# Memory keys projected by token instead of by head, and the fourth tile of x loaded one to two memory slices earlier

## The chip, the cores and the metric

One core of one Trainium2 chip. The time is that of one execution on the device in microseconds (us); of several runs the median is given. Engines are called TensorE (PE in the profile, PEld for its weight loads), VectorE (DVE), ScalarE (ACT), GpSimd (POOL) and SyncE (SP). Every engine runs its instructions in the order in which they stand in its queue, and an instruction that waits holds up those behind it.

## What is computed

One layer of a decoder trunk over 1024 tokens of width 2048, in float32. The part that the change touches is group C, in which 4 heads attend to 256 memory tokens:

```
h = rmsnorm(x, ln_g[l]);  proj = h @ w_in[l]
... groups A (spatial gating) and B (gated delta rule) ...
m = rmsnorm(mem, mem_norm_g[l])
mk, mv = jnp.split(m @ w_mem_kv[l], 2, axis=-1)      # 256 x 512 each
scores = einsum('bshd,bmhd->bhsm', cq, mk) * XA_HEAD_DIM ** -0.5
out_c = einsum('bhsm,bmhd->bshd', softmax(scores), mv) * silu(c_z)
x = x + concat(out_a, out_b, out_c) @ w_out[l];  return rmsnorm(x, final_g)
```

## The kernel before

Each float32 operand of a large product is split into a high part, rounded to TensorE's faster float32 form, and the remainder. `triple` makes one product of three matmuls: high by high, high by low, low by high.

The kernel does not issue instructions where they are written. A planner (`Plan`, `issue`) records them, prices each one with a table of costs, runs a simulated clock and puts them into each engine's queue in the order in which they would become ready, with a rank to choose between those that are ready together. So a small edit moves instructions that it doesn't name.

The first stage, some 70 us, projects the memory. For each of 16 slices `k` of the width, `load_kv` brings 128 rows of `w_mem_kv` (512 KB; four buffers: `wraw` twice, `ut` twice), ScalarE scales and casts them to `whi`, and VectorE forms `wlo`. The columns 0 to 511 of a slice make the keys, 512 to 1023 the values. `mh` and `ml` (tiles `gt` and `inv`) are the high and low parts of the transposed memory. Values are made by token: the memory is the stationary operand, two tiles `va[mt]` of 128 tokens by 512 columns (PSUM banks `dn` 0 and 1; the profile writes such a matmul `dn<-whi,gt`). Keys are made by head: the weights are stationary, four tiles `ka[h]` of 128 channels by 256 tokens, in the PSUM banks `acc` 0 to 3 (`acc<-gt,whi`). That is the layout which the attention needs, with channels on the partitions. Since a key's token then lies along the free dimension, the row scale of the memory's norm, `rm`, has to be spread over all partitions: `dg` is a diagonal of it, a product with `ones` makes `rmb`, and VectorE multiplies the four tiles with it. The results are stored (`kv_d`) by DMAs that GpSimd issues.

Between the slices the first tiles of x are prepared. `load_x` issues four loads of 128 tokens through SP, each held back by `behind(...)` until a given memory slice has been multiplied (`kvmark`). `prep` takes the row scale (squares on ScalarE, a small sum on VectorE, an inverse square root on GpSimd), scales the tile, and TensorE transposes it in four groups of four 128 x 128 pieces into two PSUM banks used in turn (`spare`: `dn` 2 and 3); VectorE multiplies them by the norm's gain into `tn`, and the high and low parts go to `ahi` and `alo`. The fourth tile, `x_rows[3]`, lies in the buffers `qT` and `qTw`. For the first two tiles `decay_rows` also makes the sums for the decay, in a free part of a bank (`first_ab`): columns 256 to 383 of `acc` 0 and 1, which the keys leave free. After that the input projection begins, which uses all banks.

The attention stands much later, from about 1198 us on. Before it the stored keys are loaded into `gt` (`mkT`) and the values into `inv` (`mv`), by GpSimd's DMAs, and split into high and low parts.

Of the kernel before, what the change touches and what calls it, by code (L numbers as in the profile page):

```python
# [9 lines left out]
F32 = mybir.dt.float32  # L10
F32R = mybir.dt.float32r
AF = mybir.ActivationFunctionType
ALU = mybir.AluOpType
# [4 lines left out]
P = 128  # L18
D = 2048
KT = D // P  # L20
# [4 lines left out]
NMEM = 256  # L25
GW, DW, XW = 512, 1024, 512
NG, NH, NX = 4, 8, 4
# [33 lines left out]
class Plan:  # L61
# [27 lines left out]
    @contextmanager  # L89
    def rank(self, cls):  # L90
        old, self.cls = self.cls, cls
        yield
        self.cls = old

    @contextmanager
    def behind(self, op):
        old, self.gate = self.gate, op
        yield
        self.gate = old
# [204 lines left out]
def kernel(  # L304
# [21 lines left out]
    x, mem, w_in, out = x[0], mem[0], w_in[0], out[0]  # L326
# [7 lines left out]
    V, S, G, PE, Q = R.dve, R.act, R.pool, R.pe, R.sp  # L334
    rank, behind = R.rank, R.behind

    def C(shape, name, dt=F32):
        return sb.tile(list(shape), dt, name=name, tag=name)[:]

    def DT(shape, name, dt=F32):  # L340
        return dr.tile(list(shape), dt, name=name, tag=name)[:]
# [41 lines left out]
    def tok(ap):  # L383

        return ap.rearrange("p (t c) -> p t c", c=P)
# [14 lines left out]
    et = [C([P, HT], f"et{i}") for i in range(2)]  # L400
    ring = {t: Slots(t, 2, [P, HT]) for t in ("kT", "qT", "vs", "kd", "ai")}
# [10 lines left out]
    rm = [rms[:, i : i + 1] for i in range(2)]  # L412
# [5 lines left out]
    dnr = Ring("dn", 4, [P, HT], pool=ps)  # L418
# [6 lines left out]
    ident, ones, utri = (C([P, P], n) for n in ("ident", "ones", "utri"))  # L425
# [11 lines left out]
    def split_to(hi, lo, src, eng):  # L437
        S.copy(hi, src)
        eng.tensor_tensor(out=lo, in0=src, in1=hi, op=ALU.subtract)

    def mm(a, lhs, rhs, start, stop, cls=9):
        with rank(cls):
            return PE.matmul(a, lhs, rhs, start=start, stop=stop, skip_group_check=True)

    def triple(a, l, r, start, stop, cls=9):

        mm(a, l[0], r[0], start, False, cls)
        mm(a, l[0], r[1], False, False, cls)
        return mm(a, l[1], r[0], False, stop, cls)
# [28 lines left out]
    def row_tiles(tag):  # L478
        return [ring[tag](), ring[tag](), *halves(twin[tag])]

    def rows_of(d, q, tt):
        return d[2 * q : 2 * q + 2, :, tt * 2 * P : (tt + 1) * 2 * P].rearrange("j p n -> p j n")

    def twos_of(t):
        return t.rearrange("p (j n) -> p j n", j=2)
# [11 lines left out]
    def kv_parts(k):  # L497
        n = XW if k == 0 else 2 * XW
        return [slice(i, i + n) for i in range(0, 2 * XW, n)]

    def load_kv(k):
        for i, sl in enumerate(kv_parts(k)[::-1]):
            (S if (k, i) == (0, 0) else Q).dma_start(kvraw[k % 4][:, sl], w_mem_kv[k * P : (k + 1) * P, sl])

    def load_x(tt, tag, after=(None,) * 4):
        x_rows[tt] = row_tiles(tag)
        for c in range(4):
            with behind(after[c] or R.gate), rank(2.8):
                Q.dma_start(x_rows[tt][c], x[tt * P : (tt + 1) * P, c * HT : (c + 1) * HT])
# [16 lines left out]
    va, ka = dnr.bufs[0:2], acc  # L526
    flip = dnr.bufs[2:4]

    def spare():
        turn["dn"] = 1 - turn["dn"]  # L530
        return flip[turn["dn"]]
# [8 lines left out]
    pt = acc[3]  # L540
# [4 lines left out]
    def times_g(o, tp, q):  # L545
        V.tensor_tensor(out=o, in0=tp, in1=bc(gcol[:, 16 + 4 * q : 20 + 4 * q], P), op=ALU.mult)
# [26 lines left out]
    H0 = NT // 2  # L573

    def first_ab(tt):
        return ka[tt][:, NMEM : NMEM + P]

    def decay_rows(a, q, t, start):

        with R.together():  # L580
            for j in range(4):
                k = 4 * q + j
                PE.matmul(a[j * 32 : (j + 1) * 32], abw[:, k * 16 : k * 16 + 32], t[:, j],
                          start=start, stop=q == NQ - 1, skip_group_check=True)

    def put0(tt):
        def put(q, tp):
            t = tok(ring["tn"]())
            with rank(1):
                times_g(t, tp, q)  # L590
            with rank(2):
                split_to(ahq[q][:, tt], alq[q][:, tt], t, V)
            if tt < H0:
                decay_rows(first_ab(tt), q, t, False)
            with rank(5):
                Q.dma_start(rows_of(h0_d, q, tt), twos_of(t.rearrange("p k c -> p (k c)")))

        return put


    kvmark = []
# [5 lines left out]
    for k in range(KT):  # L607
        mh, ml = mhl[k // 4]
        if k >= 4:
            with rank(3):  # L610
                load_kv(k)
        hi, lo = kvhi[k % 2], kvlo[k % 2]
        with rank(2):
            for sl in kv_parts(k)[::-1]:
                raw = kvraw[k % 4][:, sl]
                if k == 0:
                    V.tensor_scalar(hi[:, sl], raw, gcol[:, k : k + 1], None, op0=ALU.mult)
                else:
                    S.activation(hi[:, sl], raw, AF.Copy, scale=gcol[:, k : k + 1])
                V.scalar_tensor_tensor(lo[:, sl], raw, gcol[:, k : k + 1], hi[:, sl], op0=ALU.mult, op1=ALU.subtract)  # L620
        kk = k % 4
        for mt in range(2):
            sl = slice(mt * P, (mt + 1) * P)
            triple(va[mt], (mh[:, kk, sl], ml[:, kk, sl]), (hi[:, XW:], lo[:, XW:]), k == 0, k == KT - 1)
        for h in range(NX):
            sl = slice(h * P, (h + 1) * P)
            triple(ka[h][:, :NMEM], (hi[:, sl], lo[:, sl]), (mh[:, kk], ml[:, kk]), k == 0, False)
        kvmark.append(R.ops[-1])
        if k == 0:
            with behind(kvmark[-1]), rank(2):  # L630
                G.dma_start(abw[:, 0 : KT * 16].rearrange("p (k c) -> p k c", c=16),
                            w_in[:, C_AB : C_AB + 16].rearrange("(k p) c -> p k c", p=P))
        if k in (1, 4, 8):
            with behind(kvmark[-1]):
                mhl.append(spread_mem(len(mhl)))
        if k == 1:
            load_x(0, "vs", kvmark[1:2] * 4)
        if k == 3:
            for mt in range(2):
                V.tensor_copy(rm[mt], row_scale(mem_rows[mt]))  # L640
        if k == 4:
            load_x(1, "kd", kvmark[4:5] * 4)
        if k == 5:
            prep(0, put0(0), spare)
        if k == 7:

            dg, rmb = (ring["E"]()[:, 0:NMEM] for _ in range(2))
            for mt in range(2):
                V.tensor_scalar(dg[:, mt * P : (mt + 1) * P], ident, rm[mt], None, op0=ALU.mult)
            pt = spare()  # L650
            PE.matmul(pt[:, 0:NMEM], ones, dg, start=True, stop=True)
            S.copy(rmb, pt[:, 0:NMEM])
        if k == 9:
            prep(1, put0(1), spare)
            load_x(2, "kT", (kvmark[6], kvmark[7], kvmark[7], kvmark[8]))
        if k == 13:
            load_x(3, "qT", (kvmark[10], kvmark[11], kvmark[11], kvmark[12]))
            with rank(2):
                prep(2, put0(2), spare, (2, 3, 0, 1))

    kv_d = DT([2, NX, P, NMEM], "kvd")
    with rank(1):
        kfs = [t[:, i * NMEM : (i + 1) * NMEM] for t in et for i in range(2)]
        for h in range(NX):
            V.tensor_tensor(out=kfs[h], in0=ka[h][:, :NMEM], in1=rmb, op=ALU.mult)
    for h in range(NX):
        with rank(2.5):
            G.dma_start(kv_d[0, h], kfs[h])
    for mt in range(2):
        t = ring[("ai", "kd")[mt]]()  # L670
        with rank(1):
            S.activation(t, va[mt], AF.Copy, scale=rm[mt])
        with rank(2.5):
            G.dma_start(kv_d[1, :, :, mt * P : (mt + 1) * P].rearrange("h p e -> p h e"), tok(t))
    with rank(2):
        prep(3, put0(3), spare, (2, 3, 0, 1))
    sums0 = ring["xr"].bufs[1][:, 0:HT]
    with rank(2):
        for tt in range(H0):
            S.copy(sums0[:, tt * P : (tt + 1) * P], first_ab(tt))  # L680
# [12 lines left out]
    with rank(3.5):  # L693
        S.activation(nal, nal, AF.Exp)
        V.tensor_scalar(nal, nal, -1.0, None, op0=ALU.mult)
        pt = dnr.bufs[3]
# [1029 lines left out]
    for n, (tag, to) in enumerate((("gt", mkT), ("inv", mv))):  # L1726
        for i in range(NX // 2):
            t = ring[tag](F32R).rearrange("p (h s m) -> p h s m", h=2, s=2)
            G.dma_start(t[:, :, 1].bitcast(F32), kv_d[n, 2 * i : 2 * i + 2].rearrange("h p m -> p h m"))
            with rank(1.5):  # L1730
                split_to(t[:, :, 0], t[:, :, 1], t[:, :, 1].bitcast(F32), V)
            to += [t[:, 0], t[:, 1]]
    xab = [heir(b, f"xa{i}", f"ut{i}", 2 * HT, F32R) for i, b in enumerate(ring["ut"].bufs)]
    xat = [t[:, i * HT : (i + 1) * HT] for t in xab for i in range(2)]
# [186 lines left out]
```

## Time and profile before

| | |
|---|---|
| median of 3 runs | 1589.88 us (1587.89 to 1590.94) |
| the profiled execution | 1590.5 us, span of its instructions 1588.7 us |
| TensorE busy | 1575.6 us, 99% of the span |
| VectorE, ScalarE, GpSimd busy | 81%, 64%, 20% |
| chain of work that ended last | TensorE 98%, DMA 1% |
| DMA | 425.77 MB, 268 GB/s over the span |
| granted TensorE clock | 0.998 |

A row of a timeline gives the start, the time to the end of its last instruction, the engine, line, operation and tiles (out<-in, buffer numbers left out), shapes and count; brackets show how long the engine had been idle and who released it. Nearly all instructions carry the planner's line, L300, so one goes by the names of the tiles. Matmuls overlap: the next one starts before the last one's end.

### The profile page before, as it was taken

To read this page: it belongs to the slowest core of one execution; us is meant where nothing else is said; L and a number is where in the kernel's file an instruction comes from. 1 tells how busy PE (TensorE), PEld (TensorE's weight loads), DVE (VectorE), ACT (ScalarE), POOL (GpSimd) and SP (SyncE) were. 2 spreads that over 40 slices of the span, in tenths; PEclk is the share of its full clock that TensorE was granted. 3 is DMA by queue.
4 is the path that set the end of the run, shared out by engine and by line. 5 is a ranking of instruction groups with operands and counts; after the bars stand their busy time and mean duration, and the time that the engine had idled before them with its cause. 6 is when DMAs were issued, how large, how long until landed. Compare 5 with 4: busy or idle time off the path is not lost.

```text
span 1588.7 us, 25645 instructions
## 1 busy us (share of the span) xinstructions
PE 1575.6 (99%) x8762; PEld 1317.2 (83%) x8762; DVE 1287.4 (81%) x1961; ACT 1016.2 (64%) x2088; POOL 311.7 (20%) x513
## 2 busy tenths in 40 slices
PE   9999999999999999999999999999999999999997
PEld 8878888888888888888888888888888888888886
DVE  5868996989899998997988776777768788688775
ACT  6762685776656788866775667766566864344355
POOL 1200042332402424235343133121000000000001
PEclk9999999999999999999999999999999999999999
DMA  8988868988679868986779775798877779688646
GB/s 305 319 279 278 274 214 306 349 303 268 199 253 345 270 215 283 357 306 219 263 233 356 240 259 188 242 327 257 283 255 260 260 238 355 198 283 294 202 146 238
DMA packets 213219, 425.77 MB, mean 268 GB/s; under 512 B 23112, under 2 KB 58672, under 8 KB 213088
## 3 DMA queue, kind: packets, MB, share of 16 engines
q1 hardware_dynamic: 190464, 367.40, 68.9%
q0 software_dynamic: 21840, 55.40, 10.5%
q8 instruction: 69, 1.13, 0.3%
q10 hardware_dynamic: 784, 1.33, 0.2%
q14 instruction: 62, 0.51, 0.1%
HBM read 335.40 MB, written 88.11 MB: 267 GB/s over the span
## 4 chain that ended last, share of the span: by engine, by line
PE 98%; DMA 1%; DVE 0%; issue 0%; ACTq 0%; ACT 0%; POOLq 0%; POOL 0%; DVEq 0%
PE acc L300 69%; PE dn L300 29%; DMA wraw<-in_w_in_dram 0%; DMA wraw<-in_w_mem_kv_dram 0%; DVE alo L300 0%; DVE zl L300 0%; ACTq L300 0%; ACT y2w L300 0%; DVE tn L300 0%; DVE kd L300 0%; DVE vs L300 0%; DVE inv L300 0%; POOLq L1916 0%; POOL small L300 0%; DVE whi L300 0%
## 5 line engine op out<-in xcount | busy, mean ns | idle before, releaser
L300 PE MATMUL acc<-ahi,whi 128*128 128x512 f32 (+1 forms) x1328 | 455.6, 392 | 0.0
L300 PE MATMUL acc<-ahi,wlo 128*128 128x512 f32 (+1 forms) x904 | 355.0, 393 | 0.0
L300 PEld LDWEIGHTS acc<-ahi,whi 128*128 128x128 f32 x1328 | 247.8, 188 | 47.7
L300 ACT CAST ahi<-raws 128x1024 fp32r<-128x1024 f32 x141 | 147.9, 1049 | 86.7 <-PE dn L300 40.4
L300 PEld LDWEIGHTS acc<-ahi,wlo 128*128 128x128 f32 x904 | 170.0, 188 | 32.6 <-issue 0.2
L300 PE MATMUL acc<-alo,whi 128*128 128x512 f32 (+1 forms) x480 | 187.5, 391 | 0.0
L300 PE MATMUL acc<-ahi,zh 128*128 128x512 f32 x424 | 167.2, 394 | 0.0
L300 PE MATMUL acc<-ahi,zl 128*128 128x512 f32 x424 | 167.2, 394 | 0.0
L300 PE MATMUL acc<-alo,zh 128*128 128x512 f32 x424 | 167.1, 394 | 0.0
L300 ACT CAST whi<-wraw 128x1024 fp32r<-128x1024 f32 (+1 forms) x78 | 80.6, 1033 | 70.4 <-PE acc L300 42.8
L300 DVE TENSOR_TENSOR wlo<-wraw,whi 128x1024 fp32r<-128x1024 f32 (+1 forms) x78 | 93.6, 1200 | 25.5 <-ACT whi L300 22.0
L300 POOL TENSOR_TENSOR small<-small,mhalf 128x1 f32<-128x1 f32 x26 | 16.6, 643 | 491.1 <-DVE small L300 488.9
L300 DVE TENSOR_TENSOR alo<-raws,ahi 128x1024 fp32r<-128x1024 f32 x71 | 87.5, 1233 | 21.9 <-ACT ahi L300 21.7
L300 PEld LDWEIGHTS acc<-alo,whi 128*128 128x128 f32 x480 | 90.3, 188 | 17.4
L300 DVE TENSOR_TENSOR ahi<-raws,ahi 128x1024 fp32r<-128x1024 f32 x70 | 85.4, 1220 | 18.8 <-ACT ahi L300 17.3
L300 DVE TENSOR_TENSOR alo<-y,ahi 128x1024 fp32r<-128x1024 f32 x65 | 79.3, 1220 | 17.4 <-ACT ahi L300 17.1
L300 PEld LDWEIGHTS acc<-ahi,zl 128*128 128x128 f32 x424 | 79.7, 188 | 15.3
L300 PEld LDWEIGHTS acc<-ahi,zh 128*128 128x128 f32 x424 | 79.8, 188 | 15.3
L300 PEld LDWEIGHTS acc<-alo,zh 128*128 128x128 f32 x424 | 79.7, 188 | 15.2
L300 ACT CAST ahi<-y 128x1024 fp32r<-128x1024 f32 x65 | 68.2, 1049 | 37.3 <-PE dn L300 17.6
L300 PE MATMUL dn<-whi,ahi 128*128 128x512 f32 x232 | 77.6, 389 | 0.0
L300 PE MATMUL acc<-whi,ahi 128*128 128x512 f32 x216 | 73.6, 392 | 0.0
(582 smaller groups left out, 3744.8 us busy)
## 6 DMA issues: line engine op xcount, KB each, us to landing
wraw<-in_w_in_dram SPq DMA_DIRECT2D x80, 512.0 KB, 5.1
raws<-sa SPq DMA_DIRECT2D x61, 512.0 KB, 5.3
y<-in_w_in_dram SPq DMA_DIRECT2D x40, 512.0 KB, 5.2
wraw<-in_w_out_dram SPq DMA_DIRECT2D x32, 512.0 KB, 4.9
raws<-h0d SPq DMA_DIRECT2D x29, 512.0 KB, 6.0
y<-sa SPq DMA_DIRECT2D x27, 512.0 KB, 4.8
raws<-sd SPq DMA_DIRECT2D x42, 256.0 KB, 2.9
raws<-hTd SPq DMA_DIRECT2D x16, 512.0 KB, 5.2
```

What stands on the lines that cost most here:

```text
L300: o.fn(*o.args, **o.kw)
```

## The change

Keys are made by token, as the values are: two tiles `ka[mt]` of 128 tokens by 512 columns, with three matmuls each, in `acc` 0 and 1. `acc` 2 and 3 are free, and `first_ab` moves there. The row scale is now one number for each partition, so `dg`, `rmb` and the product that spread it go, and two VectorE instructions scale the keys. They are stored by token (`key_d`). Before the attention TensorE transposes them: two groups of four 128 x 128 pieces, into banks that `dnr` gives, from which the high and low parts are taken. The values' path is the same. And the loads of `x_rows[3]` are written at slice 10, tied to slices 9, 9, 10 and 10, where they were tied to 10, 11, 11 and 12.

```
-        return ka[tt][:, NMEM : NMEM + P]
+        return ka[2 + tt][:, 0:P]
...
-                decay_rows(first_ab(tt), q, t, False)
+                decay_rows(first_ab(tt), q, t, q == 0)
...
-        for h in range(NX):
-            sl = slice(h * P, (h + 1) * P)
-            triple(ka[h][:, :NMEM], (hi[:, sl], lo[:, sl]), (mh[:, kk], ml[:, kk]), k == 0, False)
+        for mt in range(2):
+            sl = slice(mt * P, (mt + 1) * P)
+            triple(ka[mt], (mh[:, kk, sl], ml[:, kk, sl]), (hi[:, 0:XW], lo[:, 0:XW]), k == 0, k == KT - 1)
...
-        if k == 7:
-
-            dg, rmb = (ring["E"]()[:, 0:NMEM] for _ in range(2))
-            for mt in range(2):
-                V.tensor_scalar(dg[:, mt * P : (mt + 1) * P], ident, rm[mt], None, op0=ALU.mult)
-            pt = spare()
-            PE.matmul(pt[:, 0:NMEM], ones, dg, start=True, stop=True)
-            S.copy(rmb, pt[:, 0:NMEM])
...
+        if k == 10:
+            load_x(3, "qT", (kvmark[9], kvmark[9], kvmark[10], kvmark[10]))
         if k == 13:
-            load_x(3, "qT", (kvmark[10], kvmark[11], kvmark[11], kvmark[12]))
...
-        for h in range(NX):
-            V.tensor_tensor(out=kfs[h], in0=ka[h][:, :NMEM], in1=rmb, op=ALU.mult)
-    for h in range(NX):
+    for mt in range(2):
+        with rank(1):
+            V.tensor_scalar(et[mt], ka[mt], rm[mt], None, op0=ALU.mult)
         with rank(2.5):
-            G.dma_start(kv_d[0, h], kfs[h])
+            G.dma_start(key_d[mt], et[mt])
...
+            if n == 0:
+                G.dma_start(raw, key_d[:, :, i * NMEM : (i + 1) * NMEM].rearrange("t p c -> p t c"))
+                d = dnr()
+                with rank(1.5):
+                    for h in range(2):
+                        for m in range(2):
+                            PE.transpose(d[:, (2 * h + m) * P : (2 * h + m + 1) * P], raw[:, m, h * P : (h + 1) * P], ident)
+                src = d.rearrange("p (h m) -> p h m", h=2)
```

What the planner makes of it, at three places. TensorE, one memory slice, the third (tiles 113 to 116 are the banks `acc`, 117 and 118 `dn` 0 and 1). Before:

```order
L300 MATMUL dn_118<-whi_73,inv_133 128x512
L300 MATMUL acc_113<-gt_132,whi_73 128x256
L300 MATMUL acc_113<-inv_133,whi_73 128x256
L300 MATMUL acc_113<-gt_132,wlo_75 128x256
L300 MATMUL acc_114<-gt_132,whi_73 128x256
L300 MATMUL acc_114<-inv_133,whi_73 128x256
L300 MATMUL acc_114<-gt_132,wlo_75 128x256
```

and on in the same way for 115 and 116. Now:

```order
L300 MATMUL dn_118<-whi_73,inv_133 128x512
L300 MATMUL acc_113<-whi_73,gt_132 128x512
L300 MATMUL acc_113<-wlo_75,gt_132 128x512
L300 MATMUL acc_113<-whi_73,inv_133 128x512
L300 MATMUL acc_114<-whi_73,gt_132 128x512
L300 MATMUL acc_114<-wlo_75,gt_132 128x512
L300 MATMUL acc_114<-whi_73,inv_133 128x512
```

Twelve matmuls of 256 columns in four banks have become these six of 512 in two.

TensorE, the transposes of the fourth tile of x, in the beginning of the input projection (matmuls of `ahi` and `alo`; 119 and 120 are `dn` 2 and 3). Before:

```order
L300 MATMUL dn_118<-ahi_65,wlo_76 128x256
L300 MATMUL dn_120<-ident,qTw 128x128 x4
L300 MATMUL dn_119<-ident,qTw 128x128 x4
L300 MATMUL dn_120<-ident,qT_146 128x128 x4
L300 MATMUL dn_119<-ident,qT_147 128x128 x4
L300 MATMUL acc_113<-ahi_65,inv_362 128x256
```

and now:

```order
L300 MATMUL dn_118<-ahi_65,whi_73 128x256
L300 MATMUL dn_119<-ident,qTw 128x128 x4
L300 MATMUL dn_118<-alo_69,whi_73 128x256
L300 MATMUL dn_118<-ahi_65,wlo_75 128x256
L300 MATMUL acc_113<-ahi_65,whi_74 128x256
L300 MATMUL dn_120<-ident,qTw 128x128 x4
L300 MATMUL acc_113<-alo_69,whi_74 128x256
```

The four groups no longer stand in one row: two are shown, the third and the fourth follow 12 and 23 rows behind the second. The first now stands 34 narrow matmuls behind the last matmul of the keys, where it stood behind 54.

ScalarE, the end of the memory's slices (`whi_73` from `ut_84` is slice 14, from `wraw_71` with 1024 columns slice 12; `jk` takes the squares of x's fourth tile). Before:

```order
L300 CAST ahi_65<-tn_88 128x512
L300 ACTIVATE whi_73<-ut_84,gcol 128x1024
L300 CAST ahi_66<-tn_89 128x512
L300 ACTIVATE jk,small_110<-qT_147 128x512
L300 CAST inv_362<-wraw_71 128x768
L300 ACTIVATE whi_74<-ut_85,gcol 128x1024
```

and now:

```order
L300 ACTIVATE jk,small_110<-qTw 128x1024
L300 ACTIVATE kdw<-kdw,small_108 128x512
L300 ACTIVATE whi_73<-ut_84,gcol 128x1024
L300 CAST ahi_65<-tn_90 128x512
L300 CAST inv_363<-wraw_71 128x768
```

All squares of that tile now stand ahead of the casts of slices 14 and 15.

More of the change, by code (lines that the diff above doesn't have):

```diff
@@ L655 @@
             load_x(2, "kT", (kvmark[6], kvmark[7], kvmark[7], kvmark[8]))
+        if k == 10:
+            load_x(3, "qT", (kvmark[9], kvmark[9], kvmark[10], kvmark[10]))
         if k == 13:
-            load_x(3, "qT", (kvmark[10], kvmark[11], kvmark[11], kvmark[12]))
             with rank(2):
                 prep(2, put0(2), spare, (2, 3, 0, 1))
-    kv_d = DT([2, NX, P, NMEM], "kvd")
-    with rank(1):
-        kfs = [t[:, i * NMEM : (i + 1) * NMEM] for t in et for i in range(2)]
-        for h in range(NX):
-            V.tensor_tensor(out=kfs[h], in0=ka[h][:, :NMEM], in1=rmb, op=ALU.mult)
-    for h in range(NX):
+    kv_d = DT([NX, P, NMEM], "kvd")
+    key_d = DT([2, P, XW], "keyd")
+    for mt in range(2):
+        with rank(1):
+            V.tensor_scalar(et[mt], ka[mt], rm[mt], None, op0=ALU.mult)
         with rank(2.5):
-            G.dma_start(kv_d[0, h], kfs[h])
+            G.dma_start(key_d[mt], et[mt])
     for mt in range(2):
@@ L673 @@
         with rank(2.5):
-            G.dma_start(kv_d[1, :, :, mt * P : (mt + 1) * P].rearrange("h p e -> p h e"), tok(t))
+            G.dma_start(kv_d[:, :, mt * P : (mt + 1) * P].rearrange("h p e -> p h e"), tok(t))
     with rank(2):
@@ L1728 @@
             t = ring[tag](F32R).rearrange("p (h s m) -> p h s m", h=2, s=2)
-            G.dma_start(t[:, :, 1].bitcast(F32), kv_d[n, 2 * i : 2 * i + 2].rearrange("h p m -> p h m"))
+            raw = t[:, :, 1].bitcast(F32)
+            if n == 0:
[6 more added lines that the diff above has]
+                src = d.rearrange("p (h m) -> p h m", h=2)
+            else:
+                G.dma_start(raw, kv_d[2 * i : 2 * i + 2].rearrange("h p m -> p h m"))
+                src = raw
             with rank(1.5):
-                split_to(t[:, :, 0], t[:, :, 1], t[:, :, 1].bitcast(F32), V)
+                split_to(t[:, :, 0], t[:, :, 1], src, V)
             to += [t[:, 0], t[:, 1]]
```

## Prediction

> **What bounds the kernel now.** I read the page's chain of work first, then the table of TensorE's waits, then the two stretches that the change touches, instruction by instruction.
>
> ```profile
> PE 98%; DMA 1%; DVE 0%; issue 0%; ACTq 0%; ACT 0%; POOLq 0%; POOL 0%; DVEq 0%
> PE dn L300 <- POOL ones L300: 1.1, 1, 1.1
> PE dn L300 <- DVE whi L300: 0.8, 1, 0.8
> PE dn L300 <- DVE ai L300: 0.6, 1, 0.6
> PE dn L300 <- DVE tn L300: 0.3, 1, 0.3
> PE dn L300 <- DVE inv L300: 0.2, 1, 0.2
> 60.00:80.00 20.00, 19.65 (x151) 18.50 (x150) 18.37 (x37) 14.95 (x26) 6.12 (x9) 1.00 1.05 393
> ```
>
> The reader is to see that TensorE carries 98% of the chain and that its five waits sum to 3.0 us in the whole run. So what counts is how long TensorE's own queue is, and whether the change opens a wait in it. Of the five waits one, 0.3 us for `tn`, stands where the change moves things; it is the missing 0.35 us in the stretch from 60 to 80 us (first column TensorE, then weight loads, VectorE, ScalarE, GpSimd, granted clock, DMA share, GB/s). Since matmuls overlap, a matmul's price here is the distance between starts, not the duration in the second column of a timeline. The sum is made against the profiled execution, 1590.5 us (span 1588.7), which lies 0.6 us above the median of the three runs, 1589.88.
>
> **The keys' matmuls.** The order of both programs differs only in the first sixth or so and around the attention; everywhere else it is the same. In each of 16 slices of memory, twelve matmuls of 256 columns become six of 512.
>
> ```profile
> 18.96 0.28 PE L300 MATMUL acc<-gt,whi 128*128 128x256 f32 x1
> ...
> 20.27 0.29 PE L300 MATMUL acc<-gt,wlo 128*128 128x256 f32 x1
> 20.40 0.40 PE L300 MATMUL dn<-whi,gt 128*128 128x512 f32 x1
> ...
> 21.57 0.39 PE L300 MATMUL dn<-whi,inv 128*128 128x512 f32 x1
> 21.80 0.28 PE L300 MATMUL acc<-gt,whi 128*128 128x256 f32 x1
> ```
>
> Twelve narrow ones (first and last shown) take 20.40 - 18.96 = 1.44 us, six wide ones 21.80 - 20.40 = 1.40 us: 0.04 us a slice. The first two slices run at about half pace:
>
> ```profile
> 7.87 1.19 PE L300 MATMUL dn<-whi,gt 128*128 128x512 f32 x2 [0.82 <-DVE whi L300]
> 10.56 1.05 PE L300 MATMUL acc<-inv,whi 128*128 128x256 f32 x4
> 11.42 0.63 PE L300 MATMUL dn<-wlo,gt 128*128 128x512 f32 x1
> ...
> 12.27 0.63 PE L300 MATMUL dn<-wlo,gt 128*128 128x512 f32 x1
> 13.88 0.62 PE L300 MATMUL dn<-whi,gt 128*128 128x512 f32 x2
> ```
>
> There four narrow ones take 0.86 us (10.56 to 11.42) and two wide ones 0.85 (11.42 to 12.27): nothing to gain. So 14 slices by 0.03 to 0.04 us, 0.4 to 0.6: I take **0.5 us gained**. [...]
>
> **The spread of the row scale.** The product that copied the keys' scale over all partitions goes. It is one instruction that ran as two passes:
>
> ```profile
> 38.85 0.70 PE L300 MATMUL dn<-E,ones 128*128 128x256 f32 x2
> 39.48 0.43 PE L300 MATMUL acc<-tn,abw 128*32 128x128 f32 x8
> ```
>
> From start to start 0.63 us, **0.6 us gained**. With it go two small VectorE products and a ScalarE copy, none on TensorE's path.
>
> **The transposes of the keys before the attention.** Eight are new, in two groups of four. A group of four in such a stream:
>
> ```profile
> 47.40 0.60 PE L300 MATMUL dn<-ident,kd 128*128 128x128 f32 x4
> 47.75 0.48 PE L300 MATMUL dn<-whi,inv 128*128 128x512 f32 x1
> 48.06 0.28 PE L300 MATMUL acc<-gt,whi 128*128 128x256 f32 x1
> ```
>
> The four take 0.35 us and the wide matmul behind them 0.31 instead of 0.23, so 0.43 us a group: **0.9 us lost** for two. Do they wait?
>
> ```profile
> L300 POOL DMA_DIRECT2D gt<-kvd x2: 722/742/763, 1026.6 to 1084.0; - x2
> DMA to landing us min/median/max: 4.1/7.0/7.3
> 1165.94 1.03 PE L300 MATMUL dn<-ident,vs 128*128 128x128 f32 x8
> 1166.73 0.48 PE L300 MATMUL acc<-alo,zh 128*128 128x512 f32 x1
> 1166.57 1.27 ACT L300 ACTIVATE vs<-dn,col 128x512 f32<-128x512 f32 x2 [1.59 <-PE dn L300]
> ```
>
> The keys' loads start at the latest at 1084.0 and land within 7.3 us. In the new order the new transposes follow the `vs` transposes that stand at 1165.94 by seven wide matmuls, so some 75 us after the landing; the two banks they write were read by ScalarE until 1167.84, in two equal parts, the first done near 1167.2, and the first group comes near 1168.4. No wait, by about a microsecond. The reading of the transposes replaces a reading from SBUF on ScalarE and VectorE, same number of instructions, both off the path: nothing. The four stores of scaled keys become two, and their scaling on VectorE two instructions instead of four: priced below with x's tile, which queues behind it.
>
> **The fourth tile of x.** Its four loads are released by the end of memory slices 9 and 10 instead of 10, 11 and 12, so its 16 transposes are placed in four groups between other matmuls instead of in one row. The row before:
>
> ```profile
> 75.18 1.03 PE L300 MATMUL dn<-ident,qTw 128*128 128x128 f32 x8
> 76.56 1.26 PE L300 MATMUL dn<-ident,qT 128*128 128x128 f32 x8 [0.35 <-DVE tn L300]
> 77.58 0.60 PE L300 MATMUL acc<-ahi,inv 128*128 128x256 f32 x3
> 78.02 0.31 PE L300 MATMUL acc<-alo,inv 128*128 128x256 f32 x1
> ```
>
> 2.40 us for 16, with 0.35 us of waiting for VectorE to empty the bank. Four groups at 0.43 us are 1.72: **0.7 us gained**, if the groups don't wait in their new places. The first stands 34 narrow matmuls (34 x 0.12 = 4.1 us) behind the last matmul of the keys. On VectorE its scaling stands behind the two key scalings, a `tn` and an `alo`:
>
> ```profile
> 67.85 1.50 DVE L300 TENSOR_TENSOR et<-acc,E 128x256 f32<-128x256 f32 x4 [0.19 <-PE acc L300]
> 69.87 0.68 DVE L300 TENSOR_TENSOR tn<-dn,gcol 128x512 f32<-128x512 f32 x1
> 73.41 0.88 DVE L300 TENSOR_SCALAR qTw<-qTw,small 128x512 f32<-128x512 f32 x2 [0.46 <-POOL small L300]
> ```
>
> A key scaling over 512 elements isn't in the trace; between the scaling from SBUF (`qTw`, 0.44 a piece) and the product from PSUM (`tn`, 0.68), I take the dearer, since it reads PSUM too. With `alo`, of the same size, at the same 0.68, that is 2 x 0.68 + 0.68 + 0.68 + 0.44 = 3.2 us against 4.1: free by 0.9 us; at the cheaper end by 1.4. The 0.46 us of waiting for GpSimd came from its square root standing behind the stores of keys and values; now it stands ahead of them. If every group waited as the one did, 4 x 0.35 = 1.4 us of gain would be lost; if none does, 0.7 is kept. The number of DMAs on SP's queue is unchanged.
>
> **The sum.** 0.5 + 0.6 + 0.7 - 0.9 = 0.9 us gained: 1590.5 - 0.9 = 1589.6 for an execution like the profiled one, and 1589.88 - 0.9 = 1589.0 for the median. The smallest change that a measurement of this kernel can tell from none is about 0.2%, 3.2 us; the three runs lie 3.1 us apart. So the forecast is no change that can be told.
>
> **Rivals.** (1) *The moved tile waits.* Four waits like the old one turn the 0.7 us gain into 0.7 lost: 1590.4 for the median. For it: VectorE is busy 18.37 of the 20 us from 60 to 80, and the margin above is under a microsecond. Against: the groups are apart, so a bank has some 2 us to be emptied (14 narrow matmuls and 4 transposes) before it is written again.
>
> (2) *The early loads starve the keys: slower.* In the new order ScalarE squares the last half of x's tile ahead of the cast of memory slice 14, and SP issues that half ahead of the load of slice 15.
>
> ```profile
> 45.11 4.03 SPq L300 DMA_DIRECT2D ut<-in_w_mem_kv_dram  x2
> 60.35 0.33 SPq L300 DMA_DIRECT2D qTw<-in_x_dram  x1
> DMA to landing us min/median/max: 5.3/5.6/6.1
> 49.92 0.39 PE L300 MATMUL dn<-whi,gt 128*128 128x512 f32 x1
> 62.23 0.39 PE L300 MATMUL dn<-whi,gt 128*128 128x512 f32 x1
> 62.46 1.15 ACT L300 ACTIVATE whi<-ut,gcol 128x1024 fp32r<-128x1024 f32 x1
> ```
>
> Slice 10 ends where slice 11 starts, at 49.92; two issues and a landing of up to 6.1 us later it is 57. A square of this half, a scaling and the cast follow one another on ScalarE; taken at no more than the cast's 1.15 us each they end at 60.4. Slice 14's first matmul stood at 62.23, so 1.3 us are free after TensorE's own half microsecond of gain. Slice 15's load slips from some 49 to 51 at its issue, and its cast stood at 62.46: free by 5 us. To end over 0.2% slower the landing has to be late by 1.3 + 0.9 + 3.2 = 5.4 us, so it decides from a landing of 11.5 us on, nearly twice the longest seen for this tile; price there 4.1 us, 1593.1 or more.
>
> (3) *The clock drops behind transposes.* The trace has one slow stretch, from 7.87 to 13.88, in which 6.0 us went by for what takes 3.0 at full pace. Were the new transposes to bring on another such stretch, it would cost 3.0 us: 1592.0. Against: the 16 transposes at 75.18 are followed by three narrow matmuls in 0.44 us, and the 8 at 1165.94 by a wide one in 0.31, which is the ordinary step behind transposes. [...]
>
> (4) *More than the sum.* To be faster by over 0.2% the change would have to take 2.3 us more than counted, when only 0.35 us of the waits lies in its reach: 1586.5. That it doesn't do what it says is excluded by the order: 192 narrow matmuls fewer, 96 wide ones and 8 transposes more, one spread fewer.
>
> **How the numbers follow.** The forecast 0.67 (its own range 1588.0 to 1590.0: the terms' bounds of 0.2 us and the repeats); rival (1) 0.19; (2) 0.07; (3) 0.03; (4) 0.04. Predicted time 1589.0. Range 1586.8 to 1592.0: its lower end is the lowest repeat of before, 1587.89, less the 0.9 and the 0.2 of the terms' bounds; its upper end is rival (3)'s, and covers the highest repeat, 1590.94, with the 0.5 us that rival (1) lies above before. Outside stay (4), (2) and what repeats add. Faster by over 0.2%: 0.04, from (4). Slower: 0.08, from (2) and a part of (3). Within: 0.88.
>
> **What would show it.** In the profile after: six key matmuls in 1.40 us a slice; no spread at 38.85; the `qT` groups of four between narrow matmuls, each 0.43 us and without a wait; two `gt` groups near 1167, followed at once by matmuls 0.23 us apart. Wrong would be a wait of TensorE for `whi` between 55 and 65 us (rival 2), for `qTw`, `qT` or `tn` near 70 (rival 1), or spacings of 0.42 us behind transposes (rival 3).

## The result, and the profile after

The changed kernel is slower: 1593.43 us median of 8 runs (1591.17 to 1596.79) against 1588.38 us for the kernel before beside it, a ratio of 1.0029 with a 95% interval of 1.002 to 1.0039. The forecast was 1589.0 with a range up to 1592.0. The profiled execution took 1595.3 us (span 1593.6, granted clock 0.995 instead of 0.998).

TensorE's four longest waits after (engine, tile and who is waited for: us in total, times, longest):

```profile
PE acc L300 <- DVE wlo L300: 1.7, 1, 1.7
PE acc L300 <- ACT whi L300: 1.7, 1, 1.7
PE dn L300 <- DVE whi L300: 1.4, 1, 1.4
PE dn L300 <- POOL ones L300: 1.1, 1, 1.1
```

The first two are new. To see where time went, the same three places are looked up in both timelines: the first matmul of the third memory slice, the first of the input projection, and one near 205 us. From the second to the third both kernels have the same matmuls to do. Before:

```profile
17.49 0.48 PE L300 MATMUL dn<-whi,gt 128*128 128x512 f32 x1
...
68.73 0.28 PE L300 MATMUL dn<-ahi,inv 128*128 128x256 f32 x1
...
204.45 0.39 PE L300 MATMUL acc<-ahi,wlo 128*128 128x512 f32 x1
```

After:

```profile
16.33 0.48 PE L300 MATMUL dn<-whi,gt 128*128 128x512 f32 x1
...
66.97 0.28 PE L300 MATMUL acc<-ahi,inv 128*128 128x256 f32 x1
...
209.58 0.39 PE L300 MATMUL acc<-ahi,wlo 128*128 128x512 f32 x1
```

The memory's projection ends 1.76 us sooner; 1.16 of these stand already at the third slice. Then the same work takes 209.58 - 66.97 = 142.61 us instead of 135.72: 6.89 us lost in this one stretch. Behind it the two run in step, but for 0.96 us at the keys' transposes, and 1.1 us that the changed kernel gains near 625, where it lacks two small waits of before: -1.76 + 6.89 - 1.1 + 0.96 = 5.0, the difference of the spans (4.9). So all of the loss lies in the beginning of the input projection, on whose matmuls the change has no line.

Both new waits stand there (a row's brackets: how long idle, and who released it):

```profile
79.09 0.74 PE L300 MATMUL acc<-ahi,wlo 128*128 128x256 f32 x4 [1.74 <-DVE wlo L300]
...
167.81 0.50 PE L300 MATMUL acc<-ahi,whi 128*128 128x512 f32 x1 [1.72 <-ACT whi L300]
```

And each costs nearly twice its length, as the windows behind them show (third-last column: granted TensorE clock):

```profile
79.70:83.10 3.40, 3.40 (x19) 3.40 (x18) 2.27 (x10) 2.99 (x7) 1.67 (x3) 0.50 1.06 378
...
168.50:171.90 3.40, 3.40 (x10) 2.72 (x10) 3.33 (x5) 2.91 (x4) 0.00 (x0) 0.51 1.05 375
```

From 79.09 us on 21 narrow matmuls take 4.10 us, where the step of 0.119 behind them gives 2.51; from 168.57 on 8 wide ones take 3.44, where the step of 0.233 behind them gives 1.86. So each stretch at half clock cost 1.6 us, and two waits of 1.7 and two such stretches are 6.6 of the 6.89 us. (The stretch holds two smaller terms besides, which nearly cancel: 0.65 us gained at the transposes of x's fourth tile, and some 0.6 us lost in steps that are drawn out between 159.7 and 162.1 us. Some 0.3 us stay unexplained.)

Who is late? For the first wait VectorE's and SP's queues tell it:

```profile
76.87 0.69 DVE L300 TENSOR_TENSOR tn<-dn,gcol 128x512 f32<-128x512 f32 x1 [2.54 <-DMA h0d<-tn]
...
78.08 0.95 DVE L300 TENSOR_TENSOR wlo<-wsbt,whi 128x768 fp32r<-128x768 f32 x1
```

```profile
68.06 0.42 SPq L300 DMA_DIRECT2D h0d<-tn  x1
DMA to landing us min/median/max: 3.8/6.4/8.7
```

The last line is that of the twelve such stores issued between 50 and 86 us; this one is the longest. The `tn` of x's fourth tile reuses one of four buffers, whose store to `h0d` landed only 8.7 us after its issue; the `tn` starts 0.1 us later. The `wlo` that TensorE needs stands behind that `tn`.

For the second wait the same chain is shown in both kernels: SP's load of `kTw`, and VectorE's addition that uses it. Before:

```profile
155.72 0.84 SPq L300 DMA_DIRECT2D kTw<-in_w_in_dram  x2
```

```profile
161.03 0.96 DVE L300 TENSOR_TENSOR wraw<-kTw,wraw 128x768 f32<-128x768 f32 x1
```

After:

```profile
159.82 1.99 SPq L300 DMA_DIRECT2D kTw<-in_w_in_dram  x2
```

```profile
163.64 1.55 DVE L300 SCALAR_TENSOR_TENSOR sct<-sct 128x32 f32<-128x32 f32 x7
165.22 0.19 DVE L300 SCALAR_TENSOR_TENSOR sc<-sct,sc 128x32 f32<-128x32 f32 x1
165.87 0.96 DVE L300 TENSOR_TENSOR wraw<-kTw,wraw 128x768 f32<-128x768 f32 x1 [0.46 <-DMA kTw<-in_w_in_dram]
```

The load is issued 4.1 us later and used 4.8 us later, while TensorE is only 1 us later; seven small `sct` instructions that were spread around the addition now stand ahead of it. VectorE was late before that: its previous addition from `kTw` stands at 157.46 us instead of 154.73, 2.7 us later, and it too waited for its load.

### The profile page after: what moved, and what is told of

The parts are those of the page before. It is cut to its first block, busy times and chain, and to the rows that moved or that the text cites. A ratio compares the mean times of both kernels' runs of the same rounds, so it can differ in the third digit from the quotient of the medians.

```text
span 1593.6 us, 25448 instructions
## 1 busy us (share of the span) xinstructions
PE 1577.3 (99%) x8672; PEld 1313.3 (82%) x8672; DVE 1287.1 (81%) x1957; ACT 1015.5 (64%) x2087; POOL 308.2 (19%) x511
## 3 DMA queue, kind: packets, MB, share of 16 engines
q8 instruction: 68, 1.11, 0.3%
## 4 chain that ended last, share of the span: by engine, by line
PE 92%; DMA 4%; DVE 2%; issue 1%; ACT 0%; POOL 0%; SPq 0%; ACTq 0%; POOLq 0%; DVEq 0%
PE acc L300 64%; PE dn L300 27%; DMA wraw<-in_w_in_dram 1%; DMA kTw<-in_w_in_dram 1%; DVE alo L300 1%; DMA h0d<-tn 1%; DMA kTw<-in_x_dram 0%; DMA vsw<-sa 0%; DMA wraw<-in_w_mem_kv_dram 0%; DVE wlo L300 0%; DVE wraw L300 0%; DMA y<-in_w_in_dram 0%; DVE zl L300 0%; DVE tn L300 0%; ACT whi L300 0%
```

## The experiments

All results are ratios of times to the kernel before on the same chip, with 95% intervals, from five rounds each unless said otherwise. A profile is one execution.

**Keys alone, loads alone.** The first guess, theory A, was that the early loads of x's tile make both waits. The changed kernel with the old marks:

```
-        if k == 10:
-            load_x(3, "qT", (kvmark[9], kvmark[9], kvmark[10], kvmark[10]))
         if k == 13:
+            load_x(3, "qT", (kvmark[10], kvmark[11], kvmark[11], kvmark[12]))
```

> The changed kernel with the loads of x's fourth tile back at the old marks (memory slices 10, 11, 11, 12). Theory A (the moved loads bring the changed kernel's first wait of 1.74 us at 77 us, and the delay from there brings the second, 1.72 us at 166 us; each costs about 2 us of idle and 1.9 us of halved clock): neither wait is there, and the time is before's less 1.8 us at the end of the memory's projection plus 1.0 us for the transposes ahead of the attention, about 1587.6 us, ratio to before 0.9995. Theory B (the keys by token shift the planner's clock by some 1.9 us, and it is that shift that re-orders the input projection): a wait of over 1 us stands between 70 and 210 us, and the time is 1591 to 1595.

and the kernel before with only the marks changed, the same lines the other way round:

> The kernel before with only the loads of x's fourth tile moved (slices 9, 9, 10, 10); keys by head as before. Theory A (the moved loads bring the waits): a wait of TensorE of 1 us or more near 77 us for a remainder of weights that VectorE makes behind a tn, and the time is 1591 to 1595. Theory B (the shift by the keys brings them): no such wait, 0.7 us gained where the tile's transposes stood in a row, 1587.5 to 1588.5.

Keys alone: 1.0026 (1.0015 to 1.0037). Loads alone: 1.000 (0.9991 to 1.0009). Theory A is refuted; the whole loss comes with the keys, as theory B had it. The 0.7 us that theory B expected of the loads alone did not show: a wait of 1.07 us for ScalarE's `inv` stands at 85 us in that profile. And with the keys alone the waits are others: TensorE waits at the transposes of x's fourth tile and just behind them, four times within five microseconds, 2.3 us in all (first and last), and the narrow matmuls behind them keep their full step (four in 0.47 us, from 76.30):

```profile
72.50 0.66 PE L300 MATMUL dn<-ident,qTw 128*128 128x128 f32 x4 [0.67 <-DVE qTw L300]
...
76.07 0.39 PE L300 MATMUL acc<-ahi,inv 128*128 128x256 f32 x1 [0.93 <-ACT ahi L300]
```

**One wait taken away.** In the changed kernel's queues single instructions are moved, all else left: `wlo` ahead of the `tn` that blocked it; and, apart from that, the load of `kTw` ahead of two stores and a load on SP, with its addition ahead of the seven `sct`. In short, with the names for the planner's numbers:

```
         self.ops.sort(key=lambda o: (o.at, o.idx))
+        # first kernel
+        move(wlo, ahead_of=tn)
+        # second kernel
+        move(load_kTw, ahead_of=store_pd)
+        move(wraw, ahead_of=sct)
```

> The changed kernel; in VectorE's queue the remainder wlo<-wsbt,whi is put ahead of the tn that waits for a store, so that TensorE's first wait (1.74 us) has lost what it waits for; nothing else is moved. Theory 1 (the two waits are independent): first wait and the slow matmuls behind it gone, 3.9 us gained, 1589.5. Theory 2 (what ends the second wait is a load that doesn't follow TensorE): TensorE reaches it 3.9 us sooner, the second wait grows from 1.7 to about 5.6 us, and only the halved clock of the first is saved: 1.9 us gained, 1591.5. If the first wait stays for another reason, 1593.4.

> The changed kernel; SP's load kTw that ends the second wait is put ahead of two stores and a load (issued 1.3 us sooner at most, since its buffer is read until 158.4), and on VectorE its addition ahead of the seven small sct instructions. Theory 1 (the place in SP's and VectorE's queues makes the second wait): the wait falls from 1.72 to 0.4 us or less. If a wait that short brings no slow clock, 1.3 + 1.9 = 3.2 us are gained, 1590.2. Theory 2 (the transfers themselves are behind, the 16 engines being full): the load lands no sooner and nothing is gained, 1593.4.

Both times no gain can be told: 1.0029 (1.0018 to 1.004) and 1.0029 (1.0018 to 1.004). In the first kernel the wait at 77 us is gone and the second is longer, which is the direction of theory 2. But it grew to 1.93 us, not to the 5.6 that theory 2 said, and the 1.9 us that it expected to gain did not show:

```profile
163.86 0.51 PE L304 MATMUL acc<-ahi,whi 128*128 128x512 f32 x1 [1.93 <-ACT whi L304]
```

In the second kernel the wait fell to 0.68 us and two others took its place, for `sc`, which now stood behind, and for `wlo`:

```profile
163.08 0.51 PE L304 MATMUL acc<-ahi,whi 128*128 128x512 f32 x1 [0.68 <-ACT whi L304]
164.08 0.41 PE L304 MATMUL dn<-sc,utri 128*128 128x32 f32 x2 [0.49 <-DVE sc L304]
...
165.82 0.50 PE L304 MATMUL acc<-ahi,wlo 128*128 128x512 f32 x1 [0.56 <-DVE wlo L304]
```

0.68 + 0.49 + 0.56 = 1.73 us where there had been 1.72, and the stretch at half clock followed all the same (granted clock 0.50 from 166.4 to 169.8 us). Theory 1 of this experiment (0.4 us or less, and 3.2 us gained) falls here: what was taken from one wait came back in the next two, both for VectorE. (The wait at 77 us was not in this execution, though nothing ahead of it was changed.)

**Order against instructions.** Theory O says that the keys cost nothing and the new order costs all; theory K that TensorE, arriving sooner, runs into weights that don't come sooner. A table gives every instruction the row that the same instruction has in the other kernel, and the planner's order is replaced by it, as far as data allow:

```
-        self.ops.sort(key=lambda o: (o.at, o.idx))
+        self.ops.sort(key=lambda o: place[o.idx])
```

The first kernel has the change's instructions, with the loads at the old marks, in before's order; the second has before's instructions, with the loads at the new marks, in the change's order. (The loads alone were worth nothing, as shown above.)

> Keys by token and the eight transposes, loads of x's fourth tile at the old marks, but every engine's queue in the order of the kernel before (the six wide matmuls of a slice where the twelve narrow ones stood, the rest of the five queues word for word as before up to the attention). Theory O (the loss is all in the new order that the planner made of the input projection): no wait of over 0.7 us between 70 and 210 us, and the gain that was forecast shows, about 1 us less 0.2: 1.0 us below before, ratio 0.9990 to 0.9997. Theory K (the keys themselves cost it: TensorE arrives 1.8 us sooner at weights that don't come sooner): waits with halved clock stay, ratio 1.002 to 1.003.

> The other corner: keys by head as before, no transposes before the attention, but the queues in the order of the changed kernel (with the early loads of x's fourth tile). Theory O (the order costs it): the wait of some 1.7 us near 166 us with slow matmuls behind it is there, ratio 1.002 to 1.004. Theory K (the keys themselves): TensorE isn't ahead any more, no such wait, ratio 0.9995 to 1.0005.

New instructions, old order: 0.9999 (0.9991 to 1.0008). Old instructions, new order: 1.0037 (1.0025 to 1.005). The loss goes with the order in both corners, as theory O said. The old instructions in the new order wait at the two places of the changed kernel:

```profile
80.86 0.38 PE L621 MATMUL acc<-ahi,wlo 128*128 128x256 f32 x1 [1.03 <-DVE wlo L621]
...
167.33 0.51 PE L621 MATMUL acc<-ahi,whi 128*128 128x512 f32 x1 [1.10 <-ACT whi L621]
```

They are 0.6 to 0.7 us shorter there than in the changed kernel's profile, and, against theory O, no half clock shows behind them: the granted clock of this run is 0.998, as in the kernel before, and of the 2.91 us that the table below gives to the new order 2.13 are these two waits. That fits a part of theory K, that arriving sooner lengthens a wait which the order has made, but it is one execution of each, and this one was the fastest of its six (1592.34 us, the median is 1594.63). What the slower ones lost besides is not seen.

The new instructions in the old order didn't show the gain that theory O expected, and their profile shows a reason of its own. With six wide matmuls in the places of the narrow ones, `wlo` of the first slice is wanted sooner:

```profile
10.60 0.79 PE L618 MATMUL acc<-wlo,gt 128*128 128x512 f32 x1 [1.21 <-DVE wlo L618]
```

So in one more kernel the matmuls of the first two slices stand in the changed kernel's order (those that need `whi` alone first), everything else in before's:

> As the kernel with keys by token in the order of before, but the 24 matmuls of the first two memory slices in the changed kernel's own order (the four that need only whi first), so that TensorE doesn't stand 1.2 us for the first wlo at 9.4 us. Theory O (order is all that the change lost): that wait goes, no wait over 0.5 us up to 210 us, and the forecast of the matmul counts shows: 0.9 us below before, ratio 0.9985 to 0.9998. If the keys by token cost something of their own, the ratio stays at 1.000 or above.

0.9995 (0.9985 to 1.0004), 1588.67 us against 1589.20: the best of all kernels here, but too little to tell from none. At the end of the memory's projection, before and here:

```profile
64.51 0.39 PE L300 MATMUL dn<-wlo,gt 128*128 128x512 f32 x1
```

```profile
62.64 0.39 PE L618 MATMUL dn<-wlo,gt 128*128 128x512 f32 x1
```

1.87 us are gained by then, and 1.50 remain at 185 us. Most of that is luck of the start: at the first matmul of the third slice this execution is 1.11 us ahead already (17.49 in the kernel before):

```profile
16.38 0.48 PE L618 MATMUL dn<-whi,gt 128*128 128x512 f32 x1
```

Counted from that matmul to the one near 205 us, the profiles no longer depend on how long the start was slow:

| kernel | from the third slice to the matmul near 205 us |
|---|---|
| before | 186.96 us |
| new instructions, old order (both kernels) | 186.56 us |
| old instructions, new order | 189.87 us |
| the changed kernel (two executions) | 193.25 and 190.68 us |

In the old order the new instructions gain 0.4 us there; the new order costs the old instructions 2.9 us.

**How much order does a small shift move?** The planner's price of one matmul is changed, no instruction: in the kernel before narrow key matmuls at 113 ns instead of 120, in the changed kernel wide ones at 240 instead of 227.

```
+            if self.keys and out.tensor.name[:3] == "acc" and passes == 1:
+                o.cost = 0.5 * (13.3 + 512 / 2.4)    # the changed kernel: 2 * (13.3 + 256 / 2.4)
```

> The kernel before with one number of the planner changed: it prices each narrow matmul of the keys at 113 ns instead of 120, so its simulated clock is 1.3 us ahead behind the memory's projection, as with the keys by token. The instructions are the same; only their order differs. Theory O, strong form (any shift of the clock that re-orders the input projection costs about 4 us): ratio 1.002 to 1.004. Theory O, weak form (it depends on the order that comes out): anything from 0.999 to 1.004, with the waits in the profile to tell why. Theory K: 1.000.

> The changed kernel with one number of the planner changed: it prices each wide matmul of the keys at 240 ns, so that its clock behind the memory's projection is where it stood with the narrow ones (but for the 0.44 us of the spread that is gone). Same instructions, another order. If the planner's clock alone decides: an order like that of before and a ratio of 0.999 to 1.000. If the order that comes out of any small shift is a matter of chance: it can be as slow as the changed kernel, 1.002 to 1.004, and its profile shows one or two waits of 1 us or more between 70 and 210 us, at places of their own.

1.0026 (1.0015 to 1.0037), and 1.0018 (1.0009 to 1.0027). The kernel before, with all its instructions, gets about as slow as the changed one by 1.3 us on the planner's clock; and setting the clock back does not bring the old time back. The waits are again others; behind the longest of them, 2.95 us, the granted clock is 1.00 from 80.4 to 87.2 us. Before with the new price, TensorE and VectorE:

```profile
80.34 0.66 PE L303 MATMUL dn<-ident,qT 128*128 128x128 f32 x4 [2.95 <-DVE small L303]
```

```profile
79.60 0.69 DVE L303 TENSOR_TENSOR tn<-dn,gcol 128x512 f32<-128x512 f32 x1 [2.92 <-DMA h0d<-tn]
```

The profile names `small`, but that was made long before; what TensorE waits for is the bank, which VectorE can't empty because the `tn` ring waits for its store once more. So this ring has no margin in the stretch in these orders, and it depends on the order who stands behind it.

**The changed kernel once more** (one profile):

> The changed kernel itself, profiled once more, to see whether its two waits are the same in another execution. If they are fixed by the order: 1.7 us at 77 and at 166 us again, within 0.3 us. If they hang on when the transfers land: one of them is under 1 us or gone, the other there.

```profile
83.98 0.50 PE L300 MATMUL acc<-ahi,inv 128*128 128x512 f32 x1 [1.02 <-ACT inv L300]
...
166.62 0.51 PE L300 MATMUL acc<-ahi,whi 128*128 128x512 f32 x1 [1.73 <-ACT whi L300]
```

The second wait is there to 0.01 us. The first has gone elsewhere and is shorter by 0.72 us. By the table above this execution lost 2.57 us less than the first up to the matmul near 205 us; 0.72 and the 1.6 of one stretch at half clock are 2.3 of it, so an estimate is that half clock followed one wait here instead of two. So neither of the two cases that were expected came in full. The reading that fits is that the order makes the second wait, and of the first only the lack of margin. The input projection takes 140.24 us here (68.15 to 208.39), 4.52 more than before instead of 6.89.

**The clock.** A stream of wide matmuls behind the end of the kernel before, with gaps in which TensorE waits for ScalarE (one profile for each of the next two kernels):

```
+        for sizes in ((128,), (512,), (512, 128), ...):
+            gap(sizes)          # TensorE waits for copies of these sizes, one after the other
+            stream(40)          # 40 matmuls of 512 columns
```

> The kernel before with a test stream behind its last matmul: runs of 40 wide matmuls at full pace, and between them gaps in which TensorE waits for a chain of small copies on ScalarE, rising from some 0.7 to 3.5 us, the middle ones twice; then three gaps of some 0.9 us with 2, 5 or 10 matmuls between. The output isn't touched by it. Theory G (idle time of about 1.7 us within a stretch of some 3.5 us halves the clock for some 3 us): gaps under 1.5 us leave the step at 0.226 us, gaps over 1.8 us are followed by 7 to 16 steps of 0.425 us, and three gaps of 0.9 with 2 or 5 matmuls between halve it too, with 10 between not. Rival (the slow matmuls in the changed kernel come from the full DMA engines, not from the idle time): no slow step behind any gap here, where no DMA runs. The time itself is some 200 us longer by the stream and is no comparison.

No gap up to 2.10 us was followed by a slow step, and three of 0.67 us close together neither (forty matmuls took 9.35 us behind a gap of 2.10); theory G had said from 1.8 us on. A gap of 3.42 us was:

```profile
1668.57 0.33 PE L300 MATMUL dn<-ident,E 128*128 128x128 f32 x1 [2.10 <-ACT E L300]
1668.65 9.35 PE L300 MATMUL dn<-whi,ahi 128*128 128x512 f32 x40
...
1681.53 0.39 PE L300 MATMUL dn<-ident,E 128*128 128x128 f32 x1 [3.42 <-ACT E L300]
1681.62 10.97 PE L300 MATMUL dn<-whi,ahi 128*128 128x512 f32 x40
```

Forty matmuls took 1.62 us more. The rival (full DMA engines) is refuted too, as half clock came where no transfers run (0.51 from 1681.6 to 1685.0 us, at a DMA share of 0.00). Since 1.72 had been enough in the changed kernel and 2.95 not in another, the last run puts gaps of equal length at many moments (`stream(30 + i % 3)`, three lengths, twelve times each):

> The kernel before with a test stream behind its last matmul: 36 gaps between runs of 30 to 32 wide matmuls at full pace, twelve of about 1.78 us, twelve of 2.10 and twelve of some 2.5 us, so that each length falls at many moments. Theory W (the clock is decided once every 3.41 us, on a fixed grid, by whether TensorE stood idle for about half of the time since the last such moment): of the gaps of 1.78 us some half are followed by a slow stretch, of those of 2.10 some six in ten, of those of 2.5 three quarters; all slow stretches begin and end on one grid of 3.41 us, and the gaps that leave the clock alone lie across a moment of the grid. Theory L (a threshold of length between 2.10 and 3.42 us holds in a stream like this one): none of the first 24 is followed by a slow stretch, and of the last twelve all or none. The time itself is some 350 us longer by the stream and is no comparison.

Of the twelve gaps of about 1.78 us none was followed by half clock, of those of 2.10 us five of twelve, of those of 2.55 us two of twelve. Theory W had said a half, six in ten and three quarters. Two equal gaps, one with and one without (30 and 31 matmuls behind them):

```profile
1705.02 0.37 PE L300 MATMUL dn<-ident,E 128*128 128x128 f32 x1 [2.10 <-ACT E L300]
1705.10 8.68 PE L300 MATMUL dn<-whi,ahi 128*128 128x512 f32 x30
...
1715.99 0.33 PE L300 MATMUL dn<-ident,E 128*128 128x128 f32 x1 [2.10 <-ACT E L300]
1716.08 7.31 PE L300 MATMUL dn<-whi,ahi 128*128 128x512 f32 x31
```

The slow stretches, in windows:

```profile
1705.20:1708.60 3.40, 3.40 (x9) 2.63 (x9) 0.00 (x0) 0.00 (x0) 0.00 (x0) 0.50 0.00 0
...
1838.30:1841.70 3.40, 3.19 (x8) 2.59 (x9) 0.00 (x0) 0.16 (x1) 0.00 (x0) 0.50 0.00 0
```

They begin 133.1 us apart, 39 times 3.413. Laid on a grid of that step from 1705.2, all seven gaps with a slow stretch have at least 2.10 us between two moments of the grid; the others have at most 1.93: those of 1.78 are shorter than that, and into those of 2.10 and 2.55 a moment falls. The second gap shown is cut at 1715.4 into 1.5 and 0.6 us. The gaps of this run fit theory W in its form; its half (1.7 us) was too low for this stream, and with it its shares. Theory L is refuted, as gaps of one length fell on both sides.

## Why the prediction was wrong

The counted steps came out, nearly as said. **Keys' matmuls**: six wide ones take 28.44 - 27.04 = 1.40 us, as said:

```profile
27.04 0.40 PE L300 MATMUL acc<-whi,gt 128*128 128x512 f32 x1
...
28.44 0.64 PE L300 MATMUL dn<-whi,gt 128*128 128x512 f32 x2
```

**Spread**: gone. The two steps were to give 1.1 us. From the third slice to the input projection they gave 0.6 us in this execution (50.64 us instead of 51.24) and 0.8 in the second one (50.44); where the rest went is open. The other 1.16 of the 1.76 us at 67 us are luck: half pace at the start lasted longer or shorter from one execution to the next. In the kernel before the steps of wide matmuls were 0.42 to 0.43 us from 11.4 to 13.1; in the last run with gaps, which has the same instructions in the same order there, they were 0.22 to 0.24 already from 9.7 to 10.4, and its third slice began at 14.69 us instead of 17.49. In the changed kernel the granted clock was 0.50 from 8.0 to 11.4 us, and its second execution reached the third slice 1.4 us later. **Transposes of the keys**: 0.9 us were said, 0.96 came; they don't wait, and the spacing behind them is the ordinary one, so rival (3) in its form (transposes bring on a slow stretch) did not occur (first group):

```profile
1172.68 0.60 PE L300 MATMUL dn<-ident,gt 128*128 128x128 f32 x4
1173.04 0.71 PE L300 MATMUL acc<-ahi,whi 128*128 128x512 f32 x2
```

The four pieces take 0.36 us, and the two wide matmuls behind them 0.54 instead of 0.46. **The fourth tile of x**: its groups stand apart and none of them waits; 0.35 us for four (71.02 to 71.37, then 71.82 to 72.17, and so on). With the longer step behind each group that is 0.43 to 0.44 us a group, 1.75 in all instead of 2.40: the 0.7 us came too, as 0.65. The last group ends at 75.6 us, ahead of the wait.

The step that failed is the sentence "The order of both programs differs only in the first sixth or so and around the attention; everywhere else it is the same", and what was made of it: the first sixth was priced by the instructions that the change adds and removes, and its new order at nothing. The beginning of the input projection took 6.89 us more in the profiled execution and 4.52 more in the second, where 0.7 less was forecast. The kernels in exchanged order show that this is the order (1.0037 for the new order alone, 0.9999 for the new instructions alone). The profile of before had two signs. Its row from 60 to 80 us has a DMA share of 1.05 and VectorE busy 18.37 of 20 us; the prediction used the second for rival (1) alone, and the first not at all. The reading that the runs fit, though no run tests it by itself, is that with both full the old order was one in which each thing came just in time, so that 99% busy on TensorE was no sign of slack. And the prediction asked how long the loads of x's tile take to land, 5.3 to 6.1 us (6.2 to 6.4 in the changed kernel); it did not ask for the stores of `tn`, and the one that held up VectorE took 8.7 us.

Rival (1) named the right engine and nearly the right place, at 0.19, but as waits of 0.35 us for a bank of PSUM: "a bank has some 2 us to be emptied" was true and beside the point, since the four `tn` buffers behind it were the ones that were full. Rival (3) foresaw a slow stretch, at 3.0 us where one costs 1.6 as measured, but not its cause: here it follows waits, of 1.74 and 1.72 us. So in the profiled execution one wait of 1.7 us cost 3.3, and two of them were enough to leave the range. Rival (2) did not occur: no wait for `whi` between 55 and 65 us.

What stays open: which feature of the new order makes VectorE late at 160 us. Moving the two things that the trace named only moved the wait. And how much idle time brings half clock: 2.10 us between two moments of the grid in the stream, but waits of 1.72 and 1.74 us in the changed kernel, and three of 0.68, 0.49 and 0.56 us in the one with `kTw` moved. Shorter and small matmuls stand around those waits; whether that is the reason is not shown.

## What to carry to other kernels

Where a planner sets the order, an edit has two prices: that of its instructions, and that of the new order that it brings to everything behind it; the second was several times the first here (6.89 and 4.52 us in two executions, against 0.9 forecast for the instructions), and a change of one number of the planner with no change of instructions cost nearly as much (1.0026). To judge an edit, run its instructions in the old order too, by a table of places; and don't take a stretch in which VectorE and the DMA engines are both nearly full as one with slack, however small the waits of the tuned kernel are. A wait on TensorE cost nearly double in some cases here, for the clock: some of the waits of 1.7 to 2.6 us were followed by 1.6 us more, and others were not.

## What the runs showed of the hardware

In the stream a slow stretch lasted 3.4 us at a granted clock of 0.50, and cost 1.6 us (30 matmuls in 8.68 us instead of 7.08). All seven of that run fit one grid of 3.413 us: the waits that were followed by one had at least 2.10 us between two moments of it, the others at most 1.93, so that equal waits of 2.10 us cost 2.1 us or 3.7 by where they fell. The changed kernel's first profile has three stretches at 0.50 up to 210 us, from 8.01, 79.69 and 168.44 us on. They begin 71.68 and 88.75 us apart, 21 and 26 times 3.413, and its two waits of 1.74 and 1.72 us each lie between two moments of that grid. So 2.10 us of waiting were enough in five of twelve cases of the stream, and 1.72 in the changed kernel.
